# First modulation of a two-layer diffusion trunk: weight rows streamed whole, input modulated in token chunks, two column tiles multiplied together

## The chip, the core and the metric

The kernel runs on one core of a Trainium2 chip. The metric is the device time of one execution in microseconds (us). The core has a tensor engine (PE, with its weight loads shown apart as PEld), a vector engine (DVE), a scalar engine (ACT), GpSimd (POOL), and SyncE (SP), which here issues all DMA transfers. PE writes only PSUM; the other engines move results from PSUM to SBUF. Each engine executes its own list of instructions strictly in order and waits at semaphores for the others.

## What is computed

One inference step of a two-layer trunk for 1152 tokens of 1024 features: 128 prompt tokens and 1024 sample tokens, each group with its own conditioning vector. The work around the change is the beginning of the even layer:

```python
def adaln(cond, w, b):
    m = jax.nn.silu(cond) @ w + b
    shift, scale, gate = jnp.split(m, 3, axis=-1)
    return shift[:, None], scale[:, None], gate[:, None]
def modulate(x, g, shift, scale):
    return rmsnorm(x, g) * (1 + scale) + shift
...
hp = modulate(yp, norm_g_e[i], sp, scp)      # prompt tokens
hs = modulate(ys, norm_g_e[i], ss, scs)      # sample tokens
z = h @ w_in                                 # 1024 x 3328, split into bg, cg, xs, ga, q, k, v, gb
ya = bg * short_conv(cg * xs, conv_w, conv_b) * jax.nn.silu(ga)
```

Attention over q, k, v, an output projection, and an odd layer (pooling mixer) follow; the change does not touch them. The conditioning product `silu(cond) @ w` has a 1024 x 3072 matrix; the first modulation needs its first two thirds (shift and scale), 1024 x 2048 numbers or 8.4 MB. The gate third is summed later on the vector engine, beside the projections.

## The kernel before

All products are done with a split of each fp32 operand into a high part (`fp32r`, a cast) and a low part (the rest): `split` (L96-98) makes the high part by a cast on ACT and the low part by a subtraction on DVE or POOL. One product is then three matmuls (`mm3`, L194-197): high by high (L195), high by low (L196), low by high (L197). The features lie on the 128 partitions in eight tiles (`kt` 0 to 7), the tokens in three chunks of 384 columns (`c` 0 to 2).

The order of the instructions is written out by hand: each engine gets them in the order in which the Python code emits them. `later(k, f)` puts a piece of code off by k ticks, and a tick is two `mm3` of a column tile. Loads are all in SP's list. At most eight loads are under way, because SP has eight DMA semaphores: load n waits until load n - 8 has landed.

The start of the kernel before (L233-387) goes by feature tile:

- `ada_load(kt)` loads, for feature tile kt, two slices of 128 columns of the conditioning matrix, all 1024 rows of it: pieces of 512 bytes, 1 MB per tile, in two transfers (tile name `ar`, three buffers).
- `ada_hi`, `ada_lo` split it (`ah` on ACT L287; `al` half on DVE, half on POOL, L293). `rows_mm` (L303) makes 16 matmuls of 256 columns; `cols_mm` brings the resulting row back onto partitions and makes shift and scale (`sh_e`, `s1_e`) for this feature tile only.
- `rms_in` squares the token tiles (L278, ACT), and scales them (L281, DVE). `x_T` transposes the nine token tiles for this feature tile (L324); `modulate` applies scale and shift on ACT (L332, tile `ht`); `h_split` makes `hh` (a cast on DVE, L341) and `hl` (a subtraction on DVE, L342).
- `z0(kt - 1)` multiplies feature tile kt - 1 with column tile 0 (`cg`), for the three chunks.

So each turn of the loop does a feature tile from weights to product. Column tile 1 (`xs`) and the ones after it run behind the loop as ordinary column tiles: `even_tile(n)` does 72 matmuls over all tokens from the finished `hh` and `hl`, three chunks with two PSUM buffers (`acc`) in turn. What reads a chunk out of PSUM is emitted two ticks after it. Beside the column tiles `pump_ada` emits a step of the gate sums at some of the ticks; `pace` says at which (before: 2 of 3 ticks in tile 1, then 4 of 5). A step is mostly two operations of 512 columns on DVE (L432, L434); a group of 15 steps has eight of these, then two pairs of a small split (`as`) and, three steps on, two small matmuls (L450).

Of the kernel before, what the change touches and what calls it, by code (L numbers as in the profile page):

```python
# [9 lines left out]
F32 = mybir.dt.float32  # L10
# [26 lines left out]
class Clock:  # L37
    """Emission clock: work on the tensor engine ticks it, and what depends on that work is emitted ticks later."""
# [23 lines left out]
def trunk(ctx, tc, i, o):  # L62
# [81 lines left out]
    def rsqrt(r, sq, scale, n, eng=G):  # L144
        """r = 1 / sqrt(sq * scale + eps): square root, reciprocal, one Newton step"""
# [14 lines left out]
    class Stream:  # L160
# [13 lines left out]
        def split(self, upto, pieces=1):  # L174
# [43 lines left out]
    # the gates of all features and the first feature tile come before the attention, the other convolutions beside it  # L218
# [64 lines left out]
    ah, al, rw, hts, cols = {}, {}, {}, {}, {}  # L283

    def ada_hi(kt):
        ah[kt] = L.tile([P, KT, 256], F32R, tag="ah", bufs=2, name="ah")
        A.copy(ah[kt], araw[kt].rearrange("p k a c -> p k (a c)"))  # L287

    def ada_lo(kt):
        al[kt] = L.tile([P, KT, 256], F32R, tag="al", bufs=2, name="al")  # L290
        r = araw.pop(kt).rearrange("p k a c -> p k (a c)")
        for eng, ks in ((V, slice(0, 4)), (G, slice(4, KT))):
            eng.tensor_tensor(out=al[kt][:, ks], in0=r[:, ks], in1=f32(ah[kt][:, ks]), op=ALU.subtract)  # L293

    w0 = None
    a0 = [acc(CH), acc(CH), psc(CH)]

    def rows_mm(kt):
        p = po()
        h_, l_ = ah.pop(kt), al.pop(kt)  # L300
        for n, w in enumerate((h_, l_)):
            for kk in range(KT):
                T.matmul(p[:4, :256], c4[:, kk, :], w[:, kk, :], start=(n == 0 and kk == 0), stop=(n == 1 and kk == KT - 1))  # L303
        r = L.tile([4, 256], F32, tag="row", bufs=1, name="row")
        V.tensor_copy(r, p[:4, :256])
        rw[kt] = r

    def cols_mm(kt):
        r = rw.pop(kt)
        p = psc(8)  # L310
        for third in range(2):
            T.transpose(p[:, 4 * third:4 * third + 4], r[:, third * P:(third + 1) * P], ident[:4, :4])
        m = L.tile([P, 2, 2], F32, tag="m", bufs=2, name="m")
        V.reduce_sum(m, p.rearrange("p (a h c) -> p a c h", a=2, h=2), axis=AX.X)
        V.tensor_scalar(out=sh_e[:, kt, :], in0=m[:, 0, :], scalar1=colT[:, R_BE + kt:R_BE + kt + 1], scalar2=None, op0=ALU.add)
        V.tensor_scalar(out=s1_e[:, kt, :], in0=m[:, 1, :], scalar1=bp1[:, kt:kt + 1], scalar2=colT[:, R_GE + kt:R_GE + kt + 1], op0=ALU.add, op1=ALU.mult)
# [3 lines left out]
    def x_T(kt):  # L320
        for c in range(NCH):
            p = ptr([P, 3, P])
            for k in range(3):
                T.transpose(p[:, k, :], xt[3 * c + k][:, kt * P:(kt + 1) * P], ident)  # L324
            xps[kt, c] = p.rearrange("p a b -> p (a b)")

    def modulate(kt):
        ht = L.tile([P, TOK], F32, tag="ht", bufs=2, name="ht")
        for c in range(NCH):
            p = xps.pop((kt, c))  # L330
            for lo, hi, cond in (((0, P, 0), (P, CH, 1)) if c == 0 else ((0, CH, 1),)):
                A.activation(ht[:, c * CH + lo:c * CH + hi], p[:, lo:hi], AF.Identity,  # L332
                             scale=s1_e[:, kt, cond:cond + 1], bias=sh_e[:, kt, cond:cond + 1])
        hts[kt] = ht

    def h_split(kt, pieces=1):
        ht = hts.pop(kt)
        w = TOK // pieces
        for c in range(pieces):
            cs = slice(c * w, (c + 1) * w)  # L340
            V.tensor_copy(hh[:, kt, cs], ht[:, cs])  # L341
            V.tensor_tensor(out=hl[:, kt, cs], in0=ht[:, cs], in1=f32(hh[:, kt, cs]), op=ALU.subtract)  # L342

    def z0(kt):
        wh, wl = w0
        for c in range(NCH):
            sl = slice(c * CH, (c + 1) * CH)
            mm3(a0[c], kt, wh[:, kt, :], wl[:, kt, :], hh[:, kt, sl], hl[:, kt, sl], kt == 0, kt == KT - 1)

    rms_in(0)  # L350
    small_cols()
    ada_hi(0)
    ada_lo(0)
    rms_in(1)
    rows_mm(0)
    cols_mm(0)
    rms_in(2)
    ada_hi(1)
    ada_lo(1)
    ada_load(3)  # L360
    for k in range(KT + 1):
        # rows of tile k + 1, modulation of tile k, product of tile k - 1
        if k == 0:
            x_T(k)
            modulate(k)
        if k + 2 < KT:
            ada_hi(k + 2)
        if k + 1 < KT:
            rows_mm(k + 1)
            if k + 4 < KT:  # L370
                ada_load(k + 4)
        if 0 < k < KT:
            x_T(k)
            modulate(k)
        if k + 1 < KT:
            cols_mm(k + 1)
        if k + 2 < KT:
            ada_lo(k + 2)
        if k == 0:
            w0 = st_e.start(0)  # L380
        else:
            z0(k - 1)
        if k < KT:
            h_split(k, 1 if k < KT - 1 else NCH)
# [892 lines left out]
```

## Time and profile before

| | |
|---|---|
| median of 3 runs | 957.82 us (956.85 to 958.23) |
| span of the profiled execution | 955.5 us; its own run time is not listed apart, so 2.3 us lie between its span and the median |
| PE busy over the span | 911.1 us (95%) |
| DVE / ACT / POOL busy | 564.5 / 403.1 / 276.1 us |
| column tile 1 begins / column tile 2 begins | 81.10 us / 93.74 us |

A busy PE is not a PE at its peak: matmuls overlap in the records, so the number of matmuls and the distance from one start to the next say how fast it is. "PEclk" is the share of full tensor clock that was granted.

### The profile page before, as it was taken

To read this page: it belongs to the slowest core of one execution; us is meant where nothing else is said; L and a number is where in the kernel's file an instruction comes from. 1 tells how busy PE (TensorE), PEld (TensorE's weight loads), DVE (VectorE), ACT (ScalarE), POOL (GpSimd) and SP (SyncE) were. 2 spreads that over 40 slices of the span, in tenths; PEclk is the share of its full clock that TensorE was granted. 3 is DMA by queue.
4 is the path that set the end of the run, shared out by engine and by line. 5 is a ranking of instruction groups with operands and counts; after the bars stand their busy time and mean duration, and the time that the engine had idled before them with its cause. 6 is when DMAs were issued, how large, how long until landed. Compare 5 with 4: busy or idle time off the path is not lost. (4 is left out here: it accounts for less than half of the span.)

```text
span 955.5 us, 13244 instructions
## 1 busy us (share of the span) xinstructions
PE 911.1 (95%) x4986; PEld 827.7 (87%) x4986; DVE 564.5 (59%) x1029; ACT 403.1 (42%) x855; POOL 276.1 (29%) x227
## 2 busy tenths in 40 slices
PE   1779999999999999999999999998999999999998
PEld 1469998888998999999898888898999999998887
DVE  3798967686558857866624666559442644523332
ACT  6562343444466666765434444433333332320110
POOL 1541343112334443433361000135433333410000
PEclk9599999999999999999999999999999999999999
DMA  8926553221410000100143222221110244332222
GB/s 282 274 66 190 185 188 122 84 60 30 87 45 23 24 11 13 45 23 1 67 137 127 88 89 89 99 78 39 40 50 29 88 134 145 98 100 88 89 88 78
DMA packets 89999, 85.77 MB, mean 90 GB/s; under 512 B 12756, under 2 KB 69052, under 8 KB 89936
## 3 DMA queue, kind: packets, MB, share of 16 engines
q1 hardware_dynamic: 89936, 84.93, 28.8%
q8 instruction: 39, 0.64, 0.3%
q14 instruction: 24, 0.20, 0.1%
HBM read 74.27 MB, written 9.60 MB: 88 GB/s over the span
## 5 line engine op out<-in xcount | busy, mean ns | idle before, releaser
L195 PE MATMUL acc<-hh,wh 128*128 128x384 f32 x856 | 296.2, 346 | 0.0
L196 PE MATMUL acc<-hl,wh 128*128 128x384 f32 x856 | 290.0, 339 | 0.2 <-DVE hl L342 0.2
L197 PE MATMUL acc<-hh,wl 128*128 128x384 f32 x856 | 289.9, 339 | 0.0
L98 POOL TENSOR_TENSOR wl<-raw,wh 128x1024 fp32r<-128x1024 f32 (+1 forms) x38 | 93.2, 2454 | 265.1 <-ACT wh L97 258.9
L195 PEld LDWEIGHTS acc<-hh,wh 128*128 128x128 f32 x856 | 161.5, 189 | 2.8 <-issue 0.2
L196 PEld LDWEIGHTS acc<-hl,wh 128*128 128x128 f32 x856 | 161.6, 189 | 2.1 <-DVE hl L342 0.4
L197 PEld LDWEIGHTS acc<-hh,wl 128*128 128x128 f32 x856 | 161.3, 188 | 0.1
L195 PE MATMUL acc<-woh,yh 128*128 128x512 f32 (+1 forms) x296 | 116.5, 394 | 0.0
L197 PE MATMUL acc<-woh,yl 128*128 128x512 f32 (+1 forms) x296 | 115.3, 389 | 0.0
L196 PE MATMUL acc<-wol,yh 128*128 128x512 f32 (+1 forms) x296 | 115.1, 389 | 0.0
L197 PEld LDWEIGHTS acc<-woh,yl 128*128 128x128 f32 x296 | 55.7, 188 | 12.8 <-DVE yl L98 0.3
L196 PEld LDWEIGHTS acc<-wol,yh 128*128 128x128 f32 x296 | 55.8, 189 | 11.8
L195 PEld LDWEIGHTS acc<-woh,yh 128*128 128x128 f32 x296 | 55.8, 188 | 11.8
L867 POOL TENSOR_SCALAR s<-s,dn 128x512 f32<-128x512 f32 (+2 forms) x72 | 46.6, 666 | 52.5 <-DVE dn L861 33.5
L999 DVE TENSOR_TENSOR sg<-acc,gate_s 128x512 f32<-128x512 f32 (+1 forms) x33 | 22.2, 674 | 63.5 <-PE acc L197 63.5
L434 DVE SCALAR_TENSOR_TENSOR sc<-aw,sc,sc 128x512 f32<-128x512 f32 x84 | 57.0, 746 | 3.7 <-DMA aw<-in_ada_w_o 3.7
L98 DVE TENSOR_TENSOR pT<-tr,pT 128x512 fp32r<-128x512 f32 x62 | 42.1, 686 | 22.0 <-ACT pT L97 21.4
L98 POOL TENSOR_TENSOR wol<-t,woh 128x1024 fp32r<-128x1024 f32 x16 | 39.6, 2479 | 39.2 <-ACT woh L97 39.2
L841 DVE CUSTOM_DVE_ANT_0 s<-sc,mask 128x512 f32<-128x512 f32 (+2 forms) x72 | 41.4, 612 | 15.2 <-PE sc L831 12.5
L97 ACT CAST pT<-tr 128x512 fp32r<-128x512 f32 x62 | 36.1, 588 | 32.8 <-PE tr L872 32.3
L850 ACT ACTIVATE s<-s,nm 128x512 f32<-128x512 f32 (+2 forms) x72 | 47.0, 656 | 2.6 <-DVE nm L844 2.5
L1108 DVE TENSOR_TENSOR pw<-u 128x1183 f32<-128x1183 f32 x8 | 13.5, 1682 | 54.6 <-ACT u L1141 54.6
(299 smaller groups left out, 1497.1 us busy)
## 6 DMA issues: line engine op xcount, KB each, us to landing
raw<-in_w_in_e SPq DMA_DIRECT2D x20, 512.0 KB
ar<-in_ada_w_e SPq DMA_DIRECT2D x16, 512.0 KB
aw<-in_ada_w_o SPq DMA_DIRECT2D x32, 256.0 KB
raw<-in_w_in_o SPq DMA_DIRECT2D x16, 512.0 KB
y1d<-raw SPq DMA_DIRECT2D x9, 512.0 KB
raw<-y1d SPq DMA_DIRECT2D x9, 512.0 KB
aw<-in_ada_w_e SPq DMA_DIRECT2D x16, 256.0 KB
t<-in_w_out_e SPq DMA_DIRECT2D x8, 512.0 KB
```

The lines of the kernel that those rows point to most:

```text
L97: A.copy(hi, src)
L98: eng.tensor_tensor(out=lo, in0=src, in1=f32(hi), op=ALU.subtract)
L195: T.matmul(p, lh, rh, start=first, stop=False)
L196: T.matmul(p, lh, rl, start=False, stop=False)
L197: T.matmul(p, ll, rh, start=False, stop=last)
L434: V.scalar_tensor_tensor(out=self.p[cond], in0=w, scalar=c, in1=self.p[cond], op0=ALU.mult, op1=ALU.add)
L841: V.tensor_tensor_reduce(out=s[:, :nk], in0=at.pop((u, "ps", h))[:, :nk], in1=mask[:, m0:m0 + nk], op0=ALU.add, op1=ALU.max, scale=1.0, sc ...
L850: A.activation(s, s, AF.Exp, scale=0.125, bias=at[u, "nm"][:, h:h + 1], accum_out=at[u, "dn"][:, h:h + 1])
L867: G.tensor_scalar(out=s, in0=s, scalar1=at[u, "dn"][:, h:h + 1], scalar2=0.0, op0=ALU.mult, op1=ALU.add)
L999: V.tensor_tensor(out=tm, in0=p, in1=gate[:, hs], op=ALU.mult)
L1108: V.tensor_tensor(out=pw["s"][:, 0:n], in0=u[:, 0:n], in1=u[:, 1:n + 1], op=ALU.add)
```

## The change

1. `ada_load(kt)` now loads 128 whole rows of the matrix (2048 columns, 8 KB in one piece per partition, one transfer). The product sums over rows, so no shift or scale is known until the eighth row tile has been multiplied. `ada_mm` accumulates four 512-column sums in four PSUM buffers; `ada_cols` makes all shifts and scales at the end.
2. The low parts are split as 896 columns on POOL and 1152 on DVE; the last row tile in four pieces of 512, one of them on POOL.
3. SP's list begins with row tile 0, then the first three token tiles, then row tile 1; the other six token tiles come behind all row tiles and the first two weight tiles.
4. `modulate(c, kt)` goes by chunk and feature tile: ACT writes `hh` directly, DVE writes the fp32 value `ht` from the same PSUM tile, and the subtraction for `hl` alternates between DVE (even kt) and POOL (odd kt). `first_tiles` runs 24 steps (3 chunks x 8 feature tiles); each step multiplies column tiles 0 and 1 together, and transposes and modulates the slice three steps ahead. Squares and scaling of chunks 1 and 2 are emitted inside these steps.
5. The first weight tile takes the buffers of `ah` and `al`. `even_tile` starts at 2, the gate sums start with it, at 5 of 6 ticks, later 2 of 3 (before 1 of 2).

```diff
     def ada_load(kt):
-        a = L.tile([P, KT, 2, P], F32, tag="ar", bufs=3, name="ar")
-        for third in range(2):
-            c0 = third * D + kt * P
-            Q.dma_start(out=a[:, :, third, :], in_=wae[:, c0:c0 + P].rearrange("(k p) c -> p k c", p=P))
-        araw[kt] = a
+        araw[kt] = L.tile([P, 2 * D], F32, tag="ar", bufs=3, name="ar")
+        Q.dma_start(out=araw[kt], in_=wae[kt * P:(kt + 1) * P, 0:2 * D])
...
+        parts = ((0, 896, G), (896, 2 * D, V)) if kt < KT - 1 else ((0, 512, V), (512, 1024, G), (1024, 1536, V), (1536, 2 * D, V))
+        for a, b, eng in parts:
+            split(ah[kt][:, a:b], al[kt][:, a:b], r[:, a:b], eng)
...
+    def ada_mm(kt):
+        for n, w in enumerate((ah.pop(kt), al.pop(kt))):
+            for c in range(4):
+                T.matmul(pa[c][:4, :], c4[:, kt, :], w[:, c * 512:(c + 1) * 512], start=(kt == 0 and n == 0), stop=(kt == KT - 1 and n == 1))
...
+        for lo, hi, cond in (((0, P, 0), (P, CH, 1)) if c == 0 else ((0, CH, 1),)):
+            s_, b_ = s1_e[:, kt, cond:cond + 1], sh_e[:, kt, cond:cond + 1]
+            A.activation(hh[:, kt, c * CH + lo:c * CH + hi], p[:, lo:hi], AF.Identity, scale=s_, bias=b_)
+            V.tensor_scalar(out=ht[:, lo:hi], in0=p[:, lo:hi], scalar1=s_, scalar2=b_, op0=ALU.mult, op1=ALU.add)
+        cs = slice(c * CH, (c + 1) * CH)
+        (G if kt % 2 else V).tensor_tensor(out=hl[:, kt, cs], in0=ht, in1=f32(hh[:, kt, cs]), op=ALU.subtract)
...
+    for kt in range(KT):
+        if kt + 1 < KT:
+            ada_split(kt + 1)
+        if kt + 4 < KT:
+            ada_load(kt + 4)
+        elif kt + 4 == KT:
+            st_e.fetch(2)
+            x_load(1)
+            x_load(2)
+        ada_mm(kt)
...
+    st_e.split(1, home=(L, "ah", "al"))
+    w01 = [st_e.start(0)]
+    ada_cols()
...
+    def first_tiles():
+        for n in range(3):
+            modulate(*order_0[n])
+        w01.append(st_e.start(1))
+        for n, (c, kt) in enumerate(order_0):
...
+            for z, (wh, wl) in zip(a0[c], w01):
+                mm3(z, kt, wh[:, kt, :], wl[:, kt, :], hh[:, kt, sl], hl[:, kt, sl], kt == 0, kt == KT - 1)
+            if kt == KT - 1:
+                later(2, lambda c=c: first_done(c))
+            if n in (0, 1, 2, 6, 7, 8):
+                square(3 + n if n < 3 else n)
+            if n in (2, 8):
+                normed(1 if n == 2 else 2)
+            if n + 3 < len(order_0):
+                x_T(*order_0[n + 3])
+                modulate(*order_0[n + 3])
+            if n == 14:
+                st_e.split(3)
+            tick()
...
-    pace = [3, (1, 2)]
+    pace = [6, (0, 1, 2, 3, 4)]
...
-    for n in range(1, 7):
-        if n == 2:
-            pace[:] = [5, (0, 1, 2, 3)]
+    for n in range(2, 7):
...
-    pace[:] = [2, (1,)]
+    pace[:] = [3, (1, 2)]
```

Two places show how the lists of the engines move. The first is ACT's list around the first product. Before, it holds a cast of a row slice, the first weight cast (`wh`), and the modulation of whole feature tiles (`ht`):

```order
L287 CAST ah<-ar 128x2048
L97 CAST wh<-raw 128x1024
L287 CAST ah<-ar 128x2048
L332 ACTIVATE ht<-tr,sh_e,s_e 128x128
L332 ACTIVATE ht<-tr,sh_e,s_e 128x256
L332 ACTIVATE ht<-tr,sh_e,s_e 128x384 x2
```

In the changed kernel the same list, from the last row tile on, reads (L273 are the squares of token tiles 3 and 4; L307 copies the summed rows out of PSUM):

```order
L97 CAST ah<-ar 128x512 x4
L97 CAST wh<-raw 128x1024
L307 COPY row<-acc 4x512
L307 COPY row<-sc 4x512
L332 ACTIVATE hh<-tr,sh_e,s_e 128x128
L332 ACTIVATE hh<-tr,sh_e,s_e 128x256
L332 ACTIVATE hh<-tr,sh_e,s_e 128x128
L332 ACTIVATE hh<-tr,sh_e,s_e 128x256
L332 ACTIVATE hh<-tr,sh_e,s_e 128x128
L332 ACTIVATE hh<-tr,sh_e,s_e 128x256
L97 CAST wh<-raw 128x1024
L273 ACTIVATE t,ss<-X_96 128x1024
```

The cast of the second weight tile stands behind six modulations, and the squares of chunk 1 between the modulations of chunk 0.

The second place is DVE's list at column tiles 1 and 2. Before (L432, L434 gate sums; L534 product cg by xs; L98 split of a sum; L527 taps of the convolution; L540 reads a chunk of column tile 2 out of PSUM):

```order
L432 TENSOR_SCALAR sc<-aw,sc_82 128x512 x2
L434 SCALAR_TENSOR_TENSOR sc<-aw,sc_82,sc 128x512 x4
L534 TENSOR_TENSOR wide<-acc,wide 128x384
L434 SCALAR_TENSOR_TENSOR sc<-aw,sc_82,sc 128x512 x6
L534 TENSOR_TENSOR wide<-acc,wide 128x384
L434 SCALAR_TENSOR_TENSOR sc<-aw,sc_82,sc 128x512 x4
L534 TENSOR_TENSOR wide<-acc,wide 128x384
L98 TENSOR_TENSOR as<-sc,as 128x512
L527 SCALAR_TENSOR_TENSOR yc<-wide,colT,yc 128x127 x2
L527 SCALAR_TENSOR_TENSOR yc<-wide,colT,yc 128x255
L527 SCALAR_TENSOR_TENSOR yc<-wide,colT,yc 128x256
L540 TENSOR_TENSOR yc<-acc,yc 128x384
```

In the changed kernel (L419, L481, L483, L412, L425 are the same operations in the same order: product, gate sums, taps, read of column tile 2):

```order
L419 TENSOR_TENSOR wide<-acc,wide 128x384
L481 TENSOR_SCALAR sc<-aw,sc_82 128x512 x2
L483 SCALAR_TENSOR_TENSOR sc<-aw,sc_82,sc 128x512 x2
L412 SCALAR_TENSOR_TENSOR yc<-wide,colT,yc 128x127 x2
L412 SCALAR_TENSOR_TENSOR yc<-wide,colT,yc 128x255
L412 SCALAR_TENSOR_TENSOR yc<-wide,colT,yc 128x256
L483 SCALAR_TENSOR_TENSOR sc<-aw,sc_82,sc 128x512 x4
L425 TENSOR_TENSOR yc<-acc,yc 128x384
L412 SCALAR_TENSOR_TENSOR yc<-wide,colT,yc 128x384 x2
L483 SCALAR_TENSOR_TENSOR sc<-aw,sc_82,sc 128x512 x6
L425 TENSOR_TENSOR yc<-acc,yc 128x384
```

The first gate sums, which stood beside column tile 1, now stand between the taps and the reads of column tile 2.

## Rows read from the trace of the kernel before

**Rows 1.** Busy time by stage; columns as in its second line.
```profile
core 0: us, PE busy (x) PEld busy (x) DVE busy (x) ACT busy (x) POOL busy (x), PEclk, DMA share, GB/s
0.00:23.30 23.30, 4.01 (x19) 1.98 (x19) 8.87 (x28) 15.48 (x25) 3.62 (x5) 0.99 0.83 281
23.30:81.10 57.80, 46.04 (x272) 35.31 (x273) 48.74 (x68) 32.21 (x46) 25.08 (x9) 0.80 0.64 162
81.10:93.74 12.64, 12.64 (x73) 12.64 (x73) 9.84 (x16) 1.44 (x3) 2.40 (x1) 1.00 0.82 252
93.74:161.00 67.26, 66.73 (x375) 64.41 (x374) 50.04 (x77) 24.45 (x37) 26.61 (x11) 1.00 0.54 172
```

**Rows 2.** PE's waits from 93.74 us on: waited for, total us, times, longest.
```profile
PE acc L195 <- ACT zT L1158: 2.6, 1, 2.6
PE acc L196 <- POOL dl L98: 2.0, 1, 2.0
...
PE tr L450 <- ACT as L97: 1.1, 1, 1.1
```

**Rows 3.** Timeline of DVE and POOL: start us, us, instruction, idle before.
```profile
31.57 2.36 POOL L293 TENSOR_TENSOR al<-ar,ah 128x1024 fp32r<-128x1024 f32 x1 [0.31 <-ACT ah L287]
32.37 0.41 DVE L305 COPY row<-po 4x256 f32<-4x256 f32 x1 [3.34 <-PE po L303]
...
42.96 1.22 DVE L293 TENSOR_TENSOR al<-ar,ah 128x1024 fp32r<-128x1024 f32 x1
43.91 3.16 POOL L293 TENSOR_TENSOR al<-ar,ah 128x1024 fp32r<-128x1024 f32 x1 [4.28 <-DMA ar<-in_ada_w_e]
44.09 0.75 DVE L341 CAST hh<-ht 128x1152 fp32r<-128x1152 f32 x1
44.88 3.40 DVE L342 TENSOR_TENSOR hl<-ht,hh 128x1152 fp32r<-128x1152 f32 x1
```

**Rows 4.** Transfers: SP's timeline, then two stretches of one microsecond (columns as rows 1).
```profile
1.95 0.43 SPq L244 DMA_DIRECT2D X<-in_x_prompt  x1
...
5.59 0.25 SPq L131 DMA_DIRECT2D rows<-in_conv_b  x1
...
18.00:19.00 1.00, 0.79 (x4) 0.20 (x2) 0.00 (x0) 0.95 (x3) 1.00 (x1) 1.00 1.01 406
30.00:31.00 1.00, 0.55 (x3) 0.04 (x1) 0.00 (x0) 1.00 (x1) 1.00 (x1) 0.50 1.22 291
```

**Rows 5.** Groups by shape up to 100 us: busy us, mean ns, idle before.
```profile
L287 ACT CAST ah<-ar 128x2048 fp32r<-128x2048 f32 x8 | 15.3, 1907 | 8.7 <-DMA ar<-in_ada_w_e 8.7
L278 ACT ACTIVATE hl<-X 128x1024 fp32r<-128x1024 f32 x8 | 8.4, 1055 | 0.8 <-DMA X<-in_x_sample 0.5
L332 ACT ACTIVATE ht<-tr,sh_e,s_e 128x256 f32<-128x256 f32 x8 | 4.5, 557 | 0.0
L97 ACT CAST wh<-raw 128x1024 fp32r<-128x1024 f32 x4 | 4.2, 1052 | 0.0
L332 ACT ACTIVATE ht<-tr,sh_e,s_e 128x128 f32<-128x128 f32 x8 | 3.7, 457 | 19.8 <-PE tr L324 18.8 <-issue 1.0
L281 DVE TENSOR_SCALAR X<-X,rstd 128x1024 f32<-128x1024 f32 x8 | 5.6, 750 | 0.1
```

**Rows 6.** PE's timeline: nine transposes, and matmuls of a column tile.
```profile
76.39 1.03 PE L324 MATMUL tr<-ident,X 128*128 128x128 f32 x8
...
77.29 0.42 PE L195 MATMUL acc<-hh,wh 128*128 128x384 f32 x1
...
93.74 0.34 PE L195 MATMUL acc<-hh,wh 128*128 128x384 f32 x1
```

**Rows 7.** Two stretches with the granted clock (columns as rows 1).
```profile
20.30:23.30 3.00, 0.02 (x1) 0.02 (x1) 2.82 (x7) 2.72 (x6) 0.00 (x0) 0.90 1.13 325
23.30:42.30 19.00, 13.15 (x56) 7.81 (x56) 13.76 (x21) 11.17 (x16) 10.83 (x4) 0.50 1.21 290
42.30:46.70 4.40, 4.40 (x17) 3.66 (x18) 4.20 (x6) 1.54 (x1) 2.79 (x1) 0.51 0.86 215
```

**Rows 8.** DVE's timeline at column tiles 1 and 2.
```profile
83.90 1.41 DVE L432 TENSOR_SCALAR sc<-aw,sc 128x512 f32<-128x512 f32 x2 [3.21 <-DMA aw<-in_ada_w_e]
85.21 2.72 DVE L434 SCALAR_TENSOR_TENSOR sc<-aw,sc,sc 128x512 f32<-128x512 f32 x4
...
96.42 3.67 DVE L527 SCALAR_TENSOR_TENSOR yc<-wide,colT,yc 128x127 f32<-128x127 f32 x4
100.19 0.56 DVE L540 TENSOR_TENSOR yc<-acc,yc 128x384 f32<-128x384 f32 x1
```

More of the change, by code (lines that the diff above doesn't have):

```diff
@@ L172, in fetch, with split @@
                 self.n_f += 1
[L174 removed]
+        def split(self, upto, pieces=1, home=None):
             while self.n_s < min(upto, self.limit):
@@ L295, in trunk @@
[L295 to L316, printed above, removed]
@@ L350, in trunk @@
[L350 to L384, printed above, removed]
-        if k == KT - 3:
-            st_e.split(2)
+    ah, al = {}, {}
@@ new lines, in ada_cols @@
+    def ada_cols():
+        r = L.tile([4, 2 * D], F32, tag="ar", bufs=3, name="row")
+        for c in range(4):
+            dst = r[:, c * 512:(c + 1) * 512]
+            if c % 2:
+                V.tensor_copy(dst, pa[c][:4, :])
+            else:
+                A.copy(dst, pa[c][:4, :])
+        p = po()[:, :4 * 2 * KT]
+        for k in range(2 * KT):
+            T.transpose(p[:, 4 * k:4 * k + 4], r[:, k * P:(k + 1) * P], ident[:4, :4])
+        m = L.tile([P, 2 * KT, 2], F32, name="m")
+        bc = lambda ap: ap.unsqueeze(2).to_broadcast([P, KT, 2])
+        V.reduce_sum(m, p.rearrange("p (k h c) -> p k c h", h=2, c=2), axis=AX.X)
+        V.tensor_tensor(out=s1_e, in0=m[:, KT:], in1=bc(bp1), op=ALU.add)
+        V.tensor_tensor(out=s1_e, in0=s1_e, in1=bc(colT[:, R_GE:R_GE + 8]), op=ALU.mult)
+        V.tensor_tensor(out=sh_e, in0=m[:, :KT], in1=bc(colT[:, R_BE:R_BE + 8]), op=ALU.add)
@@ new lines, in trunk @@
+    ada_split(0)
+    ada_load(3)
+    small_cols()
+    for t in range(3):
+        square(t)
+    normed(0)
+    for kt in range(KT):
[8 more added lines that the diff above has]
+        ada_mm(kt)
+    order_0 = [(c, kt) for c in range(NCH) for kt in range(KT)]
+    for n in range(3):
+        x_T(*order_0[n])
+    st_e.split(1, home=(L, "ah", "al"))
@@ new lines, in trunk, with cs_, conv_cg, conv_piece @@
+    cv = {}
+    def cs_(c):
+        return slice(c * CH, (c + 1) * CH)
+    def conv_cg(j, c, z):
+        if c == 0:
+            cv["p"] = wide()
+        A.copy(cv["p"][:, cs_(c)], z)
+    def conv_piece(j, c):
+        p, y = cv["p"], yc[:, j, :]
+        w0_, w1_, w2_ = (colT[:, R_CW + 4 * k + j:R_CW + 4 * k + j + 1] for k in range(3))
+        lo, hi = c * CH, (c + 1) * CH
+        d = y[:, lo:hi] if j == 0 else half_tile()[:, :CH]
+        A.activation(d, p[:, lo:hi], AF.Identity, scale=w1_, bias=colT[:, R_CB + j:R_CB + j + 1])
+        def taps():
+            for s0, s1 in ((0, P), (P, TOK)):
+                for k, w in ((-1, w0_), (1, w2_)):
+                    a, b = max(lo, s0, s0 - k), min(hi, s1, s1 - k)
+                    if a < b:
+                        V.scalar_tensor_tensor(out=d[:, a - lo:b - lo], in0=p[:, a + k:b + k], scalar=w, in1=d[:, a - lo:b - lo], op0=ALU.mult, op1=ALU.add)
+            if j > 0:
+                V.tensor_tensor(out=y[:, lo:hi], in0=y[:, lo:hi], in1=d, op=ALU.mult)
+        later(1, taps)
@@ L573, in even_tile @@
             ztile(st_e, n, hh, hl, lambda c, z: conv_parts[part](j, c, z))
-    for c in range(NCH):
-        later(1, lambda c=c: conv_cg(0, c, a0[c]))
-    pace = [3, (1, 2)]
+    pace = [6, (0, 1, 2, 3, 4)]
     def pump_ada(t):
```

129 lines of the change are left out of this document (47 added, 82 removed).

## The prediction

> **What bounds the kernel now.** I read the busy time by stage first [rows 1]. From 81.10 us on PE is the bound: 72 matmuls of 384 columns take 12.64 us, one every 0.176 us, and from 93.74 to 161 us it is busy 66.73 of 67.26 us. Then I read the list of PE's waits from 93.74 us to the end: six short ones, 9.1 us in all, the two longest and the one that matters below shown in [rows 2]. So nothing behind the start hides a loss or a gain of the start: what counts is the time at which column tile 2 begins with tiles 0 and 1 done (93.74 us before), and whether PE runs on without waits from there.
>
> The start is not bound by PE. From 23.3 to 81.1 us PE holds 272 matmuls in 57.8 us at a mean clock of 0.80, while DVE and POOL together are busy 48.74 + 25.08 = 73.8 us, of which a part is waiting inside an instruction. That part I read in the timeline of both [rows 3]. POOL's subtraction of 1024 columns takes 2.36 us when alone. At 43.91 POOL asks while DVE subtracts; DVE's next cast still goes through (0.75 us), POOL then works until 47.07, and DVE's subtraction of 44.88 takes 3.40 us, the rest of POOL's 2.19 us and 1.21 us of its own. So two SBUF operations of DVE and POOL run one after the other, and their durations add up. DVE's copy out of PSUM at 32.37 is not held up by the POOL instruction of 31.57.
>
> **The row tiles (part A).** A DMA of wide rows (4 KB) moves 406 GB/s, the 512-byte slices 291 GB/s [rows 4]. Row tile 0: the first token tile (0.52 MB) was issued at 1.95 and landed at 5.59, when SP's next wait for it ended; twice the bytes in its place land 1.3 us later, at 6.9 us. Three token tiles at 1.3 us each: 10.8. Row tile 1 (2.6 us): 13.4. From there a row tile needs 2.6 us of transfer, and the shared work more: POOL 896 columns 896/1024 x 2.36 = 2.07 us, DVE 1152 columns 1.27 us (1024 take 1.13 from 42.96 to 44.09), in turn 3.3 us. Row tiles 1 to 6 are 20.0 us, the last one 3 x 0.57 + 1.2 = 2.9, and the scaling of the first token tiles on the same pair 3.3 (three of 0.75 [rows 5] and five small ones of some 0.2). With the first cast of 0.94 (its share of 1.9) the last low part is ready at 13.4 + 0.9 + 20.0 + 2.9 + 3.3 = 40.5 us. A load waits for the split three tiles before, 4.9 us from issue to landing by the first token tile (3.6 us, and 1.3 more): two splits of 3.3 cover it. PE's 64 matmuls of 512 columns lie beside this at either clock. Then come the last product, two copies on ACT and two on DVE, 16 tiny transposes, a sum and three small operations: 4.0 us by the durations of the same steps in the loop before. The factors are ready at 44.5 us, with 1 us for hand-overs (my estimate) at 45.5.
>
> One edge: POOL's low part of the first weight tile asks at about 40 us, before DVE's last piece. In rows 3 DVE's next instruction went first, and I sum with that. The Trainium skill, page "SBUF — State Buffer", section "Who interferes with whom", says that the one who issues first takes the pair for its whole instruction; by that POOL goes first and 2.4 us are added. The trace agrees with the exclusive use, not with the order at 43.91.
>
> **The two column tiles (part B), counted from the factors.** ACT modulates three slices, 0.76 us each (457 + 557 ns, less what overlaps), then casts the second weight tile (1.05): 3.35 us. POOL's low part of it takes 2.36: 5.75. The first step's last matmul needs it, so PE stands almost idle until 6.0. In the trace PE without work from 20.3 to 23.3 fell to half clock, and the 4.4 us of unbroken work from 42.3 brought it back [rows 7]; I take half clock from here: 0.32 us per matmul, 0.65 us for three transposes.
>
> The slice three steps ahead is transposed only behind the step (6.7), modulated (7.6), then ACT squares a token tile (1.06 and a 0.19 read: 1.2) to 8.8, next slice to 10.2, third square to 11.4, root 11.7. DVE scales chunk 1 in 3.2 us: 14.9. Only then comes the sixth slice's `ht` (0.5) and POOL's subtraction (0.9): 16.3. PE stands at step 6 for some 2 us and ends it at 17.2. At full clock a step is 6 x 0.176 + 0.3 = 1.35 us (nine transposes take 0.90 [rows 6]). Steps 7 and 8: 20.2. ACT meanwhile does three modulations of chunk 1 (0.55) and three squares: 23.0, root 23.3, DVE 3.1, `ht` and POOL's subtraction 1.4: 27.8. PE reaches step 12 at 24.5, waits 3.3 us, ends it at 28.7. The last 12 steps are 15.6 us with no scaling left in DVE's list; per two steps DVE has 1.5 us and POOL 0.9 against PE's 2.7. That gives 44.3, and 45.3 with 1 us for hand-overs. Column tile 2 begins at 45.5 + 45.3 = 90.8 us, 2.9 us earlier than 93.74.
>
> **Behind it (part C).** The gate sums now begin here. Their first load waits for PE's last use of the first weight tile, 0.5 us before tile 2, and lands some 3.2 us later, as before (DVE's wait of 3.21 [rows 8]): 2.8 us into tile 2. DVE's list then has two plus two sums (0.66 each, 5.4), four taps (1.4 without POOL in the way, which took the rest of the 3.67), four sums (9.5), and the read of tile 2's first chunk, done at 10.0. PE needs that PSUM buffer at 8.4 for chunk 2: it waits 1.6. Before, this read began 6.5 us into the tile. Two taps and six sums later the second read ends at 15.7; PE wants its buffer at 14.2: 1.5. The first split of a sum ends at 18.9, the small matmul behind it stands in PE's list at about 17.7: 1.2. Together 4.3 us. Against it, PE's wait of 1.1 us at a small matmul near 161 us [rows 2] may go, as the sums stand elsewhere: 0 to 1.4, I take 0.7. The faster pace in the q, k, v stage is free: 36 steps in place of 27 there, and DVE was 74% busy just before it [rows 1].
>
> **The sum.** -2.9 + 4.3 - 0.7 = +0.7 us, on a span of 955.5: 956.2. The median stands 2.3 us above the span, so 958.5 us. Bounds of what the trace does not show: the 384-column `ht` from PSUM between 0.4 (the copy at 32.37) and 0.7 us on 24 steps of slack; hand-overs 0 to 5 us; part A by the order of POOL 0 to 2.4; part C 2 to 6 us.
>
> **Rivals.**
> *DVE is not late (faster).* The sums of part C fit between, because PE's list needs the reads later than I count, or the loads land earlier; the scaling steps in part B then cost less too, if POOL's and DVE's turns interleave well. For it: before, DVE is at 9.84 of 12.64 us in tile 1 and PE never waited. Against: the two reads stand behind eight more sums. Without the 4.3 us: 954.2 us; with half of the two waits at steps 6 and 12 also gone, 951.6.
> *The clock falls at each wait (slower).* PE has three waits in part B, and one step in half clock costs 2.6 us in place of 1.35. If the waits at steps 6 and 12 let the clock fall again, each costs 2.2 us (4.4 us of work at half speed), and with POOL first at 40 us (2.4) the sum is +7.5: 965; with one of the three 961. It decides the sign as soon as the clock stands at half (1.2 GHz) behind either of the two: 2.2 us more is beyond what a measurement can miss. The Trainium skill, page "TensorE: Matmul & The Clock Gate", section "HAM oscillation — how this bites in real kernels", has this as its rule: bursts with waits between them start each time at half rate. By that rule both waits count, 963 us; the trace agrees for the one at 23 us.
> *The change saves nothing at the start* since the factors now come only after all eight row tiles: that holds if a row tile's transfer takes the 291 GB/s rate and 3.6 us; the shared pair then still hides most of it, and part A ends 2 us later: 960.5. The row of wide pieces speaks against it.
>
> **How the numbers follow.** The sum as it stands, 955.5 to 961: 0.50. DVE not late: 0.22. Clock falls or POOL first: 0.22. The late start: 0.06. A difference of 0.2% (1.9 us) is about what a measurement can tell from none. Faster by more: 0.20 from the first rival and 0.10 from the sum's lower edge, 0.30. Slower by more: 0.20 from the clock, 0.04 from the late start, 0.15 from the sum's upper edge, 0.39. Within: 0.31. The range 952.5 to 964 leaves out the far ends of both rivals.
>
> **What would show it.** In the profile after: DVE and POOL in turn up to 40 to 43 us, with no transfer waited for after row tile 2; the first matmul of the column tiles at about 46 us and PE idle until 51; PE waiting for POOL's or DVE's `hl` near 61 and 73 us; tile 2 at 89 to 93 us; then three waits of PE for DVE within 20 us. If tile 2 begins before 87 us, parts A or B are wrong; if PE has no wait in tiles 2 and 3, part C is.

## The result and the profile after

The changed kernel takes 972.51 us (median of 4 runs, 972.26 to 973.85); the kernel before, run beside it, 957.83 us (956.85 to 958.23). The ratio is 1.016, with a 95% interval of 1.0146 to 1.0175. The forecast was 958.5 us with a range of 952.5 to 964: the change is slower, by more than the range allowed. The profiled execution has a span of 970.5 us, 15.0 more than before.

Where the 15.0 us are follows from three landmarks that both kernels have: the products of q (first to last), those of the attention weights with the values, and those of the odd layer's pooling mixer. First the kernel before, then the changed one; the times after the durations are the start of the first and of the last instruction.

```profile
L195 PE MATMUL acc<-wq_h,hh x72: 393/396/398, 162.6 to 237.2; 128*128 128x512 f32 x72
L887 PE MATMUL po<-pT,vt x124: 387/393/502, 278.3 to 466.3; 128*128 128x512 f32 x124
L196 PE MATMUL acc<-dl,pmh x48: 336/336/525, 662.9 to 760.0; 128*128 128x384 f32 x48
```
```profile
L196 PE MATMUL acc<-wq_h,hh x72: 391/396/398, 171.6 to 246.2; 128*128 128x512 f32 x72
L886 PE MATMUL po<-pT,vt x124: 387/393/507, 294.8 to 482.9; 128*128 128x512 f32 x124
L197 PE MATMUL acc<-dl,pmh x48: 336/336/443, 679.4 to 775.0; 128*128 128x384 f32 x48
```

With the first matmul of column tile 2 (93.74 us before [rows 6], 101.07 us after, below), the differences are:

| stretch | before | after | difference |
|---|---|---|---|
| start to column tile 2 | 93.74 | 101.07 | +7.3 |
| column tile 2 to first q product | 68.9 | 70.5 | +1.7 |
| first to last q product | 74.6 | 74.6 | 0 |
| last q product to first value product | 41.1 | 48.6 | +7.5 |
| first value product to first pooling product | 384.6 | 384.6 | 0 |
| first to last pooling product | 97.1 | 95.6 | -1.5 |
| the rest | 195.5 | 195.5 | 0 |

The -1.5 goes with a stretch of lower clock (0.83 from 670 to 680 us) that only the profiled execution of the kernel before has. Two losses are to be explained: 7.3 us at the start, 7.5 us behind q, k, v.

The busy time by stage answers to [rows 1]. The columns are busy us and instructions of PE, PEld, DVE, ACT, POOL, then the granted clock and the DMA.

```profile
23.00:46.70 23.70, 15.43 (x69) 6.25 (x69) 18.27 (x14) 10.64 (x14) 14.18 (x7) 0.93 0.97 351
46.70:56.70 10.00, 4.04 (x10) 2.55 (x11) 3.83 (x9) 4.83 (x9) 3.36 (x2) 0.50 0.16 43
56.70:68.00 11.30, 7.67 (x38) 6.98 (x37) 6.84 (x18) 6.48 (x14) 2.01 (x2) 0.80 0.15 45
68.00:74.67 6.67, 6.67 (x27) 6.44 (x27) 3.67 (x7) 3.88 (x7) 1.04 (x2) 0.56 0.00 0
74.67:88.00 13.33, 10.75 (x71) 10.26 (x70) 9.96 (x21) 6.93 (x14) 3.98 (x4) 1.00 0.00 1
88.00:101.07 13.07, 11.73 (x70) 10.37 (x68) 9.28 (x13) 5.93 (x11) 6.39 (x5) 1.00 0.26 81
```

The first row is the row tiles, with the DMA engines busy 0.97 of the time. Then the factors are there (46.73 us), and in the ten microseconds in which the two column tiles should get going no engine is busy even half of the time. An idle PE beside idle DVE, ACT and POOL, with the DMA at 0.16, means that they wait for each other. The timeline of all engines in that place shows how:

```profile
46.83 0.46 ACT L332 ACTIVATE hh<-tr,sh_e,s_e 128x128 fp32r<-128x128 f32 x1 [6.21 <-DVE sh_e L316]
47.32 0.41 DVE L333 TENSOR_SCALAR ht<-tr,s_e,sh_e 128x128 f32<-128x128 f32 x1 [0.59 <-ACT hh L332]
47.77 0.91 ACT L332 ACTIVATE hh<-tr,sh_e,s_e 128x256 fp32r<-128x256 f32 x2 [0.48 <-DVE ht L333]
48.37 0.54 DVE L333 TENSOR_SCALAR ht<-tr,s_e,sh_e 128x256 f32<-128x256 f32 x1 [0.64 <-ACT hh L332]
48.38 0.69 PE L196 MATMUL acc<-hh,wh 128*128 128x384 f32 x1 [2.42 <-ACT hh L332]
48.95 0.56 DVE L335 TENSOR_TENSOR hl<-ht,hh 128x384 fp32r<-128x384 f32 x1
49.42 0.41 DVE L333 TENSOR_SCALAR ht<-tr,s_e,sh_e 128x128 f32<-128x128 f32 x1
49.86 0.57 ACT L332 ACTIVATE hh<-tr,sh_e,s_e 128x256 fp32r<-128x256 f32 x1 [1.18 <-DVE ht L333]
```

`hh` (ACT) and `ht` (DVE) are both computed from the same PSUM tile `tr` and write different tiles; neither needs the other's result. (In both traces only ACT and DVE take results out of PSUM, POOL never does.) Yet each of the two waits for the other: ACT's piece of 128 columns, then DVE's 128, ACT's 256, DVE's 256. The program's own lists say so: DVE's `ht` has a wait for ACT's counter, ACT's second `hh` of a slice one for DVE's. Over all 24 slices DVE stood idle for ACT's `hh` 16 times before an `ht`, 15.8 us in all, and ACT eight times for DVE's `ht`, 8.2 us. In the last two rows `hl` of the first slice, which PE needs, holds DVE up, and ACT waits 1.18 us for its turn at the second slice. ACT comes through three slices in 5.1 us, at 51.9.

PE's waits from 46 to 104 us (us in total, times, longest):

```profile
PE acc L196 <- ACT hh L332: 4.8, 2, 2.4
PE sc L197 <- POOL hl L335: 2.6, 1, 2.6
PE acc L196 <- ACT wh L97: 2.3, 1, 2.3
PE acc L197 <- POOL hl L335: 1.5, 2, 1.2
PE acc L197 <- DVE hl L335: 1.5, 2, 1.0
PE acc L198 <- POOL wl L98: 1.4, 1, 1.4
```

14.1 us in all. Three of them in PE's timeline, and the first product of column tile 2 as the last row:

```profile
66.32 0.44 PE L196 MATMUL acc<-hh,wh 128*128 128x384 f32 x1 [2.42 <-ACT hh L332]
67.97 0.69 PE L197 MATMUL acc<-hl,wh 128*128 128x384 f32 x1 [1.21 <-POOL hl L335]
...
81.82 0.44 PE L197 MATMUL sc<-hl,wh 128*128 128x384 f32 x1 [2.58 <-POOL hl L335]
...
101.07 0.44 PE L196 MATMUL acc<-hh,wh 128*128 128x384 f32 x1
```

A first matmul behind a wait takes 0.44 us at full clock and 0.69 us at half clock: PE fell to it again at 67.97 us (0.56 in the row from 68.00). (The prediction counts steps from one: its step 6 is n = 5 in the code, its step 12 is n = 11; the expectations of the kernels with early sums or squares name n.)

Behind q, k, v the last four small products of the gate sums stand in PE's list:

```profile
250.45 0.40 PE L499 MATMUL tr<-as,onesr 128*2 128x512 f32 x1 [1.94 <-ACT as L97]
251.17 0.45 PE L499 MATMUL tr<-as,onesr 128*2 128x512 f32 x1 [0.33 <-DVE as L98]
...
253.98 0.63 PE L499 MATMUL tr<-as,onesr 128*2 128x512 f32 x1
255.90 0.39 PE L499 MATMUL tr<-as,onesr 128*2 128x512 f32 x1 [1.29 <-DVE as L98]
```

In the kernel before all these stood ahead of 237 us:

```profile
161.61 0.40 PE L450 MATMUL tr<-as,onesr 128*2 128x512 f32 x1 [1.14 <-ACT as L97]
...
236.01 0.62 PE L450 MATMUL tr<-as,onesr 128*2 128x512 f32 x2
```

The change leaves fewer ticks before the end of q, k, v (the 12 of tile 1 are gone). There are 90 steps. The changed kernel has 50 places for them in the column tiles and 36 in q, k, v. One more step goes between the two stages, where the program emits steps until the buffers that hold loaded rows are empty, and three are left, which are emitted at once behind q, k, v. The kernel before has even fewer places, 56 and 27, but eight steps go between the stages there (the small products around 161.61 us are part of them), and nothing is left. The waits behind q, k, v and one of 0.86 us for DVE at 267 us are 4.4 us, the four products 1.9, and 12 matmuls of k and v follow each other at 0.21 us instead of 0.12, 1.1 us (the clock is 0.50 from 251.4 to 254 us): 7.4 of the 7.5.

### The profile page after: what moved, and what is told of

Its sections match the earlier page's. It is cut to its first block, busy times and chain, and to the rows that moved or that the text cites. A ratio compares the mean times of both kernels' runs of the same rounds, so it can differ in the third digit from the quotient of the medians.

```text
span 970.5 us, 13117 instructions
## 1 busy us (share of the span) xinstructions
PE 913.8 (94%) x4922; PEld 822.6 (85%) x4922; DVE 569.5 (59%) x1029; ACT 406.4 (42%) x867; POOL 279.7 (29%) x239
## 5 line engine op out<-in xcount | busy, mean ns | idle before, releaser
L98 POOL TENSOR_TENSOR wl<-raw,wh 128x1024 fp32r<-128x1024 f32 (+1 forms) x38 | 93.2, 2456 | 246.6 <-ACT wh L97 246.3
L483 DVE SCALAR_TENSOR_TENSOR sc<-aw,sc,sc 128x512 f32<-128x512 f32 x84 | 57.1, 744 | 3.7 <-DMA aw<-in_ada_w_o 3.6
L98 DVE TENSOR_TENSOR pT<-tr,pT 128x512 fp32r<-128x512 f32 x62 | 42.1, 685 | 22.1 <-ACT pT L97 21.5
L98 POOL TENSOR_TENSOR wol<-t,woh 128x1024 fp32r<-128x1024 f32 x16 | 39.6, 2480 | 38.3 <-ACT woh L97 38.3
L97 ACT CAST pT<-tr 128x512 fp32r<-128x512 f32 x62 | 36.1, 587 | 32.9 <-PE tr L871 32.3
```

What stands on the lines that cost most here:

```text
L97: A.copy(hi, src)
L98: eng.tensor_tensor(out=lo, in0=src, in1=f32(hi), op=ALU.subtract)
L483: V.scalar_tensor_tensor(out=self.p[cond], in0=w, scalar=c, in1=self.p[cond], op0=ALU.mult, op1=ALU.add)
```

## The experiments

Diffs are against the changed kernel. "Tile 2" is the time of the first matmul of column tile 2.

**One reader of PSUM.** ACT writes `ht`, DVE casts `hh` from it.

```diff
-            A.activation(hh[...], p[:, lo:hi], AF.Identity, scale=s_, bias=b_)
-            V.tensor_scalar(out=ht[:, lo:hi], in0=p[:, lo:hi], scalar1=s_, ...)
+            A.activation(ht[:, lo:hi], p[:, lo:hi], AF.Identity, scale=s_, bias=b_)
+        V.tensor_copy(hh[:, kt, cs], ht)
```


> In the changed kernel ACT (hh) and DVE (ht) both read a slice's PSUM tile and take turns; here ACT alone reads it (ht), DVE casts hh from ht in SBUF. Theory A (the taking of turns makes the column tiles long): the second weight tile's low part is ready at about 53 us instead of 55.4, the first three slices are through ACT by 49.7, the wait at step 6 shrinks from 4.6 to about 2 us; column tile 2 begins at 94 to 97 us instead of 101.1, and the time is 965 to 969 us. Theory B (the scaling of token chunks 1 and 2 between the slices, and the clock that falls at each wait, make it long): hh still stands behind the scaling in DVE's list, PE stands at steps 6 and 12 as before, tile 2 begins at 100 to 102 us, 971 to 974 us.

Measured 966.97 us, ratio to before 1.0102 (1.0088 to 1.0115); tile 2 at 96.06 us. These are theory A's numbers. The waits at step 6 shrank from 2.42 and 1.21 us to 0.65 and 0.69. Behind the second scaling PE still waits, 1.84 us for DVE's `hh` and 0.64 us for POOL's `hl` instead of 2.58 us, so theory B holds a part.

**Gate sums at every tick of q, k, v.**

```diff
-    pace[:] = [3, (1, 2)]
+    pace[:] = [1, (0,)]
```


> The changed kernel with a step of the gate sums at every tick of the q, k, v stage instead of two of three. Theory A (the sums begin a column tile later and overrun the q, k, v stage; PE waits there for their small products, 4.4 us of waits and a stretch of half clock between 248 and 268 us): those four small products stand earlier, PE has no wait there, 964 to 967 us. Theory B (the waits come from DVE being late as such): more steps on DVE only move the waits to other places of the same stage, 971 to 975 us.

984.77 us, 1.029 (1.0276 to 1.0304): 12 us more than the changed kernel, outside both. PE now waits inside the stage, 9.01 us for the first of two such pairs of small products and 5.58 us for the second, and its clock falls there (0.73 from 212 to 222 us, 0.70 from 242 to 252 us):

```profile
211.73 1.31 PE L499 MATMUL tr<-as,onesr 128*2 128x512 f32 x2 [9.01 <-ACT as L97]
```

DVE was late for lack of data too: its longest wait was 5.6 us for a load, which stood in SP's list behind stores of k and v until 194.9 us. The steps stand earlier in the lists, but these two pairs weren't done earlier; only PE met them sooner.

**Second weight tile split first.**

```diff
     ada_cols()
+    w01.append(st_e.start(1))
...
         for n in range(3):
             modulate(*order_0[n])
-        w01.append(st_e.start(1))
```


> The changed kernel with the second weight tile's split (ACT 1.03 us, POOL 2.4 us) emitted before the first three slices are modulated; both engines are idle there from 41.8 to 46.8 us. Theory A (the turns of ACT and DVE set the pace, 2 us per slice): the waits of 2.35 us for wh and 1.44 us for wl go, but PE then waits for slices, and tile 2 begins 1 to 2 us earlier, 970 to 972 us. Theory B (the late second weight tile and the half clock it leaves behind set it): the steps begin 3.8 us earlier and the clock is up at step 1, tile 2 at 96 to 97 us, 967 to 968.5 us.

968.06 us, 1.0115 (1.0099 to 1.013); tile 2 at 97.0. Theory B's numbers: the late second weight tile, with the half clock behind it, cost 4.1 us at tile 2. The waits for `wh` and `wl` are gone, and the clock first comes up at 53 us, in the changed kernel at 60; how the 4.1 us divide between the two, this run doesn't tell. The wait behind the second scaling (2.6 us) is as before.

**The three together.** 

> The three edits together: one reader of PSUM, the sums at every tick of the q, k, v stage, the second weight tile split before the slices. If the three causes are separate: tile 2 begins at 91 to 94 us, no waits near 250 us, 954 to 960 us. If they hide each other: 962 to 966 us.

975.84 us, 1.0201 (1.0182 to 1.022). Tile 2 at 93.53, as expected of separate causes, though they overlap a little: 7.5 us together, 5.0 and 4.1 alone. The time was missed, since the pace of the sums costs about as much as before.

**Squares and scaling spread.** On top of one reader and the early split: 

```diff
+    for t in range(3, 6):
+        square(t)                       # ahead of the first slices
...
+        normed(1)                       # ahead of n = 0
-            if n in (0, 1, 2, 6, 7, 8):
-                square(3 + n if n < 3 else n)
-            if n in (2, 8):
-                normed(1 if n == 2 else 2)
+            if n < 3:
+                square(6 + n)
+            if n == 3:
+                roots(2)
+            if n in (3, 4, 5):
+                scaled(3 + n)
```


> The changed kernel with one reader of PSUM and the second weight tile split first, and besides: the squares of token chunk 1 are emitted before the first slices, those of chunk 2 in steps 0 to 2, and DVE scales chunk 1 before step 0 and chunk 2 one token tile per step (steps 3 to 5). The pace of the gate sums is that of the changed kernel. Theory A (what is left of the long column tiles, tile 2 at about 93.5 us with the two edits, are the blocks of squares and scaling): no wait at steps 6 and 12, one stretch of half clock only, tile 2 begins at 84 to 88 us, and the time is 956 to 960 us (972.5 less 13 to 17). Theory B (DVE is too full for two column tiles in any order): tile 2 at 91 to 94 us, 963 to 966 us.

958.23 us, 1.001 (1.0 to 1.002); tile 2 at 87.02, 14.0 us earlier than in the changed kernel. Theory A.

**The same with two readers.** Only `modulate` differs from the kernel above: it is that of the changed kernel.

> The kernel with spread squares and scaling, but with ACT and DVE both reading each PSUM tile as in the changed kernel. If the turns of the two readers cost time by themselves (two handed-over reads per slice, three slices ahead): tile 2 begins 2 to 5 us later than with one reader, 959 to 964 us. If they cost only because the scaling blocked DVE in the midst of a slice: within 1 us of the kernel with one reader.

969.77 us, 1.0131 (1.0116 to 1.0146); tile 2 at 98.15. Two readers cost 11.1 us at tile 2, more than twice the most that was expected. PE's waits up to tile 2, with one reader and then with two:

```profile
PE acc L196 <- DVE hh L340: 2.9, 2, 2.2
PE acc L197 <- POOL hl L341: 1.1, 2, 0.8
PE acc L197 <- DVE hl L341: 0.2, 1, 0.2
```
```profile
PE acc L196 <- ACT hh L338: 5.2, 3, 2.8
PE acc L197 <- POOL hl L341: 4.4, 4, 1.7
PE acc L197 <- DVE hl L341: 2.6, 4, 1.0
```

One reader also means less work for DVE: it is busy 27.0 us from 46.9 us to tile 2, with two readers 34.3. But with two it also stands idle for ACT's `hh` for 12.4 us, and ACT for DVE's `ht` for 11.0 us, eight times. So the waits between the two carry most of it, by the trace; no run separates them from the longer work.

And the place of the timeline above, with one reader (its first three slices, six pieces, take ACT 2.52 us in a row):

```profile
46.89 2.52 ACT L338 ACTIVATE ht<-tr,sh_e,s_e 128x128 f32<-128x128 f32 x6 [2.14 <-DVE sh_e L322]
47.84 0.36 DVE L340 CAST hh<-ht 128x384 fp32r<-128x384 f32 x1 [1.04 <-ACT ht L338]
48.23 0.56 DVE L341 TENSOR_TENSOR hl<-ht,hh 128x384 fp32r<-128x384 f32 x1
48.25 0.69 PE L196 MATMUL acc<-hh,wh 128*128 128x384 f32 x1 [2.22 <-DVE hh L340]
```

**More sums in tiles 2 to 6**, half the pace in q, k, v (on top of the spread kernel: `pace` 1 of 1, then 1 of 2).

> The kernel with one reader and spread scaling, with the gate sums at every tick in column tiles 2 to 6 (60 steps instead of 50) and at every second tick of the q, k, v stage (27 instead of 36). Theory A (the stage behind q, k, v loses 5 to 7 us because some of the 90 steps are left over and are emitted at once, with their small products next to each other): nothing is left over, 4 to 6 us less than with the pace of the changed kernel. Theory B (DVE has no room for it in tiles 2 to 6): waits for the reads of PSUM there grow by as much, no gain.

961.2 us, 1.0042 (1.003 to 1.0054). The stretch from first q to first value product is as before the change (115.7 us), but tile 2 to first q product takes 81.6 us instead of 71.0. Theory B.

**Three of four ticks in q, k, v** (spread kernel).

> The kernel with one reader and spread scaling, with the gate sums at three of four ticks of the q, k, v stage (40 steps instead of 36), so that none of the 90 is left over. Theory A (left-over steps): 4 to 6 us less than with two of three ticks. Theory B (the stage holds no more steps than at two of three; loads and DVE are late, as at every tick, where PE waited 9 us for one small product): as long or up to 6 us longer.

956.62 us, 0.9996 (0.9987 to 1.0004): 1.6 us below the spread kernel, between the two ranges. Nothing is left over, and in the profiled execution (958.96 us, the longest of twelve) the time from first q to first value product is 123.3 us, against 123.0: nearer to theory B. PE waits 3.6 us inside the stage instead of behind it, and falls to half clock there (0.50 from 232 to 236 us).

**Sums begun inside the column tiles**, from n = 18, and then four of them with earlier loads.

> The kernel with one reader and spread scaling, in which the gate sums begin in token chunk 2 of the two column tiles (a step after each of steps 18 to 23, six in all), with the pace of the changed kernel after that: 6 + 50 + 36 = 92 places for 90 steps, so none is left over behind q, k, v. Theory A (what the stage of q, k, v loses is the backlog of the later start of the sums): the waits for small products there and behind it go, tile 2 begins within 1 us of 87, and the time is 950 to 954 us, below the kernel before. Theory B (DVE has no room for the steps wherever they stand): the six steps push the reads and the low parts of chunk 2 back, tile 2 begins 2 to 4 us later and the time is 957 to 960 us.

> As the kernel that began the sums at step 18, but with four sums, after steps 19, 21, 22 and 23, where DVE has little left to do, and with their first loads issued at step 8, ahead of the third weight tile's (there they came behind it, and DVE waited 1.20 us for one in the midst of the slices). 4 + 50 + 36 = 90 places for 90 steps. Theory A (backlog): tile 2 begins at 87 to 89 us, no waits between 220 and 290 us, 951 to 954 us, faster than the kernel before by about 0.5%. Theory B (DVE has no room): tile 2 at 90 us or later, 957 to 960 us.

962.24 us (1.0035 to 1.0063 of before) and 961.86 us (1.0029 to 1.0054); tile 2 at 95.65 and 93.85. Neither tests what it should: both also moved DVE's work on a small constant in front of the first slice, where DVE waited 6.5 and 8.0 us for its load.

**14 of 16 products of the last two gate sums left out.**

> The changed kernel without 14 of the 16 products of row tiles in the last two gate sums (the odd layer's scale is then wrong; the loads stay): 76 steps, none left over behind q, k, v. Theory A (left-over sums cost the changed kernel 7.5 us between the last q product and the attention): column tile 2 still begins at 101 us, the distance from the last q product to the first product of the attention with the values is as in the kernel before (41 us instead of 48.6), 964 to 966 us. Theory B (that stage is long for another reason, such as the clock or the later k and v): no change beyond 1.5 us, 971 to 973 us.

969.92 us, 1.0133 (1.0113 to 1.0153). In its profiled execution, the longest of five (973.1 us), tile 2 begins at 102.8, the q products run from 173.9 to 252.0, and the first value product stands at 293.1 us. From the last q product to the first value product it is 41.1 us again, as theory A says; but the q products take 78.1 us instead of 74.6, with 2.2 us of waits for small products near 223 us. So 4.0 of the 7.5 us came back between first q and first value product, and 2.6 us in the medians, which lies outside both ranges.

**PE kept busy at the wait.** 20 matmuls that nobody reads, ahead of n = 6 and then ahead of n = 5.

```diff
+            if n == 5:
+                idle = po()
+                for k in range(20):
+                    T.matmul(idle, w01[0][0][:, 0, :], ..., start=True, stop=True)
```


> The changed kernel with 20 matmuls of 512 columns whose results nobody reads, put ahead of step 6, where PE stands from 63.6 to 68.0 us (20 x 0.213 us = 4.3 us at full clock). Theory A (the second stretch of half clock, 68.0 to 73.6 us, costs what its 24 matmuls and transposes take longer, some 2.5 us, and the wait at step 12 gives part of it back): no half clock after 66 us, tile 2 begins 0 to 2.5 us earlier, 970 to 972.5 us. Theory B (the clock that falls at the waits carries most of the loss): tile 2 begins at 96 to 97 us, 967 to 968.5 us.

> The changed kernel with the same 20 matmuls one step earlier, ahead of the sixth slice's products (n = 5), where PE really stands from 63.6 to 66.3 us and then to 68.0 us. Theory A (the second stretch of half clock costs the length of its own matmuls, some 2.5 us, and the wait of 2.6 us behind the second scaling takes part of it back): full clock from 60 us on, tile 2 begins 0 to 2.5 us earlier than 101.1, 970 to 972.5 us. Theory B (the clock that falls at the waits carries most of the loss): tile 2 at 96 to 97 us, 967 to 968.5 us.

The first stood one step behind the wait and only added work (5.98 us from 70.62 us on): 977.97 us (1.0202 to 1.0232), tile 2 at 107.28. The second took 972.06 us, 1.0146 (1.0125 to 1.0167), and in the profiled execution (972.16 us) tile 2 began at 101.02. Its clock by stretches, as above, and the product behind the second scaling:

```profile
64.00:68.00 4.00, 4.00 (x20) 3.24 (x19) 2.97 (x6) 1.27 (x3) 0.64 (x1) 1.00 0.00 0
68.00:74.67 6.67, 6.19 (x40) 5.73 (x38) 4.39 (x8) 5.47 (x11) 2.40 (x3) 1.00 0.00 0
74.67:88.00 13.33, 10.76 (x61) 10.23 (x60) 9.62 (x21) 5.59 (x11) 3.02 (x3) 0.87 0.01 1
```
```profile
80.39 0.69 PE L197 MATMUL sc<-hl,wh 128*128 128x384 f32 x1 [2.57 <-POOL hl L335]
```

The clock stays full up to that wait, which is as long as ever and ends 1.4 us earlier (80.39 for 81.82); there it falls after all, and the 1.4 us are lost again. So in this execution the second stretch of half clock is worth 1.4 of the 7.3 us: the rest of what PE loses by it, it would have waited anyway. That is theory A for this execution, but not for all: two of the five took 969.23 and 966.81 us, at a mean clock of 0.989 and 0.993 over the span where the other three had 0.986 to 0.988. The four of the changed kernel lie between 972.26 and 973.85. There is no trace of the two, so what the clock costs stays open, between 1.4 and some 6 us.

**Four early sums, mended.**

> As the kernel with four early sums, but the small constants' loads and DVE's work on them stand behind the column tiles again, as in the changed kernel (there DVE waited 8.0 us for one of them in front of the first slice, which spoilt that kernel and the one before it). Theory A (backlog): tile 2 begins at 87 to 89 us, nothing is waited for between 220 and 290 us, and the time is 954 to 957 us, 1 to 4 us below the kernel with spread scaling. Theory B (DVE has no room for the sums in this half wherever they stand; what is saved behind q, k, v is lost in column tiles 2 to 6): tile 2 to the first q product takes 73 to 75 us in place of 71, and the time is 957 to 959 us, as with spread scaling alone.

955.05 us, ratio 0.9979 (0.997 to 0.9988): faster than the kernel before by 0.2%, the one version that is. Tile 2 at 87.73.

```profile
L196 PE MATMUL acc<-wq_h,hh x72: 392/396/398, 162.0 to 236.6; 128*128 128x512 f32 x72
L905 PE MATMUL po<-pT,vt x124: 387/393/501, 277.7 to 465.7; 128*128 128x512 f32 x124
```

41.1 us from the last q product to the first value product, no wait from 168 to 300 us: the 7.3 us of the spread kernel at that place were the backlog. Its time and its waits are theory A's. Tile 2 to first q product is 74.3 us instead of 71.0, as theory B says: PE waits 3.03 us there at 99.83 us for a read by DVE, with the clock at 0.52 from 101 to 104 us. So 3.3 of the 7.3 us went to the tiles; tile 2 itself begins 0.7 later, and the span is 3.3 us shorter. The four early sums do more than fill four places: eight steps now go between the stages instead of one, as in the kernel before, and only 28 are left for q, k, v.

## Why the prediction was wrong

The span was forecast 0.7 us longer and is 15.0 us longer. The 14.3 us between are +1.2 in part A, +9.0 in part B, -1.9 in part C up to the first q product, +7.5 behind q, k, v, and the -1.5 of the odd layer.

*Part A was right to 1.2 us, by two errors of opposite sign.* The factors came at 46.73 us, 45.5 were forecast. The edge went the other way: POOL's low part of the first weight tile got in front of DVE's last piece.

```profile
39.13 2.63 POOL L98 TENSOR_TENSOR wl<-raw,wh 128x1024 fp32r<-128x1024 f32 x1
```

PE's last matmul of a row tile waited 2.35 us for that piece, at 42.36. That is the 2.4 us that the prediction had set apart for it, and the order that the Trainium skill ("SBUF — State Buffer", "Who interferes with whom") gives; the row at 43.91 of [rows 3], on which the sum was made, did not repeat itself. The rest of part A took 1.2 us less than its sum. One sign named for it failed: ACT still waited 1.45 us for the load of row tile 5, at 29.67 us.

*Part B failed in its first term: "ACT modulates three slices, 0.76 us each (457 + 557 ns, less what overlaps)".* A slice took ACT 1.70 us, because DVE's reads of the same tile stand between ACT's. The diff shows two operations on one PSUM tile, and the lists of the program showed the waits; I had priced both operations and not their order. At n = 5 the same order cost more: ACT began 128 columns at 62.13 us and could not go on until DVE, which had the scaling of a chunk in front of its turn, had read them:

```profile
65.70 0.91 ACT L332 ACTIVATE hh<-tr,sh_e,s_e 128x256 fp32r<-128x256 f32 x2 [3.12 <-DVE ht L333]
```

So step 6 ended 23.0 us behind the factors (17.2 forecast), step 12 36.1 (28.7), and tile 2 began 54.3 us behind them (45.3). That two readers carry a large part of these 9.0 us is shown by the changed kernel with one reader, whose tile 2 begins 5.0 us earlier, and by the pair of spread kernels, 11.1 us apart. How the other 4.0 us divide no run shows; spreading the squares and scaling, on top of one reader and the early split, brought 6.5 us more, but those blocks were in the forecast's sum. The waits named in the forecast, at steps 6 and 12, were there, and the second one had its size (2.6 us, 3.3 forecast).

*The clock rival* was right on what happens; its price isn't borne out by the one trace that tests it. The clock fell at the start and behind step 6 (0.56 in 68.00:74.67), not behind step 12 of this execution. The Trainium skill's rule on bursts ("TensorE: Matmul & The Clock Gate", "HAM oscillation — how this bites in real kernels") holds for two of three waits. The rival priced a fall at 2.2 us; in the one trace with busy matmuls the second fall is worth 1.4 us, and two faster executions without a trace leave open whether it can be more.

*Part C*: the waits came where the forecast put them, in the reads of `bg` and at a small product,

```profile
110.73 0.44 PE L196 MATMUL acc<-hh,wh 128*128 128x384 f32 x1 [0.97 <-DVE yc L425]
116.42 0.41 PE L196 MATMUL acc<-hh,wh 128*128 128x384 f32 x1 [1.19 <-DVE yc L425]
119.57 0.39 PE L499 MATMUL tr<-as,onesr 128*2 128x512 f32 x1 [0.33 <-DVE as L98]
```

2.5 us for the three instead of 4.3, and the wait near 161 us [rows 2] went, as assumed: +1.7 us up to the first q product, +3.6 forecast. (The six waits that the prediction counts behind 93.74 us are six rows of the list with seven waits; their total of 9.1 us is right.)

*"The faster pace in the q, k, v stage is free" failed outright.* The places of that stage were counted (36 for 27) and DVE's share looked at, but the 90 steps were not followed to their end: 50 + 1 + 36 are emitted in time, where the kernel before had 56 + 8 + 26. What is left over is emitted with no product of its stage between, PE waits for it, and the stretch behind q, k, v is 7.5 us longer. The runs show that no place is free: the steps cost about 7 behind q, k, v or inside it, over 10 in tiles 2 to 6 at every tick, and 3.3 when four of them stand at the end of the first two column tiles.

## What to carry to other kernels

Two engines that read one PSUM tile may be ordered one behind the other by the program itself: look for a wait between readers in the lists before pricing them side by side, and let one engine read and the other work on its copy in SBUF. In a fixed order, follow all work that runs alongside to its last step: a backlog is paid where the list runs out. A count of places is not enough: the kernel before has 83 for 90 steps and no backlog, and more places in the same stage only moved the waits into it. What helped was to begin earlier. A wait at the end of a chain on other engines is shortened in the chain: with PE kept busy ahead of it, the wait at step 12 was 2.57 us for 2.58, in the one trace there is.

## What was not expected of the hardware

Waits of equal length end at different clocks. Behind the wait at step 12, 2.58 us long in the changed kernel and 2.57 us in the one with busy matmuls, the next products took 0.34 us (full clock) and 0.52 us (half). In the odd layer both kernels wait 1.96 and then 2.64 us at the same two products; the ten microseconds behind have a granted clock of 0.83 before and 1.00 after. And of DVE and POOL, which work in SBUF one after the other, POOL went first at 39.13 us, where it had asked first, though not at 43.91 us before; there DVE's next instruction was a cast, here a subtraction, and no run separates the two. Whether the two engines could read one PSUM tile at once was not tried: the program's waits forbid it here.
